# Hybrid conv / RG-LRU block: two output tiles on half the tokens at the start, the recurrence's factors in a PSUM bank, one subtraction on VectorE

## The chip, the cores and the metric

One core of a Trainium2 chip runs the whole kernel. The time is device microseconds (us) of one execution on that core. Engines are named as in the profile: PE is TensorE (matmuls), PEld its weight load, DVE VectorE, ACT ScalarE, POOL GpSimd, SP SyncE, which here only issues DMAs (SPq in the rows).

## The reference

A decoder block on 512 tokens of width 1024, in float32. Cut to what matters for the beginning of the kernel:

```python
h = rmsnorm(x, norm1_g)                      # 512 x 1024
z = h @ w_in + b_in                          # 1024 x 6656
z_glu, z_rx, z_rg, z_ga, z_gb = split(z, (2048, 1280, 1280, 1024, 1024))
u = z_glu[:, :1024] * sigmoid(z_glu[:, 1024:])          # then a causal convolution over 31 tokens
xb = causal_conv4(z_rx) ; r, i = sigmoid(gates of xb)
a = exp(-8 * r * softplus(-lru_lambda))      # 1280 channels, one lambda each
h_t = a * h_(t-1) + sqrt(1 - a^2) * i * xb   # the recurrence
# ... two output matrices, sigmoid merge, w_mix_out, residual, rmsnorm, SwiGLU, residual, rmsnorm
```

## The kernel before

Activations lie transposed, channels on the 128 partitions and the 512 tokens along a tile of one PSUM bank. Every float32 matrix is split in a high and a low part (fp32r), and a product is three matmuls: high by high, high by low, low by high. An output tile of `w_in` (128 channels) is 8 slices of the contraction times 3, so 24 matmuls; `mm3` issues them, and with `lo_last=True` the eight with the weight's low part come after the sixteen with its high part.

A weight tile is a *chunk* of 128x1024 (512 KB). `emit_chunk` issues its load on SP into one of 4 buffers `raw`, casts it to the high part (`copy`, ACT unless VectorE is named), and subtracts for the low part (`lo`, POOL for the chunks of `w_in`), both in one of 5 buffers `hl`. `emit_to(n)` emits all chunks up to number n. The chunks come in the order in which PE wants them: 0 and 1 are the two halves of the first gated unit (GLU) tile, 2 and 3 those of the second, 4 and 5 the first tiles of the recurrent branch.

The beginning stands in one block `manual_schedule`, in which PE, ACT, DVE and SP keep the order of the code; behind it a scheduler arranges the instructions. The 512 tokens are four blocks of 128, `x[0]` to `x[3]`. `norm1_rows(t)` norms one block: ACT squares and sums both halves, DVE scales the first sum (the "stats" operation, L544), ACT takes the root, DVE the reciprocal (L551) and multiplies the two halves of x by it (L588). `turn_half(.., hf, ..)` then turns 256 tokens (two blocks) channel by channel: two transposes on PE into a bank (`tx`, L567), the high part `h1..h` by ACT (L575), the low part `h1..l` by DVE (L576), 8 times. `early_mm(i, hf)` multiplies early output tile i with half hf of the tokens; `EARLY = 2` means two GLU tiles, of two chunks each, so four output tiles on 256 tokens at a time. Later tiles are taken by `in_mm` on all 512 tokens, with the same 24 matmuls, each twice as wide.

The per-channel parameters (13 of them: gains, biases, taps, `lru_lambda`) come as short rows, are turned by PE and copied by DVE into the tile `par`: `rows_turned(c0, c1)`, whose bank is `par_ps`. `ROWS` gives their order. From `lru_lambda` some 25 tiny DVE operations (128x10) and one exponential make the factors `c4`, `c8` of the recurrence, and two make `bh`.

DMAs of SP go over eight semaphores in turn, so each waits, before it is issued, until the one eight places ahead has landed; what stands behind it on SP waits too.

Of the kernel before, what the change touches and what calls it, by code (L numbers as in the profile page):

```python
# [22 lines left out]
LRU_C = 8.0  # L23
# [4 lines left out]
NR = DR // P  # L28
# [23 lines left out]


ROWS = [
    ("norm1_g", 8), ("b_in", 52), ("conv_dw_b", 8), ("conv_ln_g", 8), ("conv_ln_b", 8),
    ("conv_b_out", 8), ("lru_conv_b", 10), ("lru_ba", 10), ("lru_bx", 10),
    ("lru_lambda", 10), ("norm2_g", 8), ("lru_conv_w", 40),
    ("conv_dw_w", 248),
]


def gate_pieces():
# [24 lines left out]
def tile_block(ctx, tc, a, out):  # L87
    nc = tc.nc
    pool = lambda name, bufs, **k: ctx.enter_context(tc.tile_pool(name=name, bufs=bufs, **k))
    consts = pool("consts", 1)  # L90
# [30 lines left out]
    def split_to(h, l, full, eng, copy=act.copy):  # L121

        copy(h, full)  # L123
# [18 lines left out]
    def wchunk(key, src, kt, cols, where="hl", lo=pool_e, after=None):  # L142
        chunks.append((key, src, kt, cols, where, lo, after))

    def emit_chunk(copy=act.copy):
        if emitted[0] == GATES_AT:
            load_gates()
        key, src, kt, cols, where, lo, after = chunks[emitted[0]]
        emitted[0] += 1
        n = kt * cols  # L150
        if where == "made":
            raw = src()
        else:
            raw = raws.tile([P, 1024], F32, tag="raw", name=f"raw_{key}")
        rv = raw[:, :n]
        if where == "made":
            pass
        elif callable(src):
            src(raw)
        else:  # L160
            newest["load"] = nc.sync.dma_start(rv.rearrange("p (k n) -> p k n", k=kt), src).ins
# [12 lines left out]
    def emit_to(n, copy=act.copy):  # L174
        while emitted[0] < min(len(chunks), n):
            emit_chunk(copy)

    def weights(key, ahead=AHEAD):
        i = next(i for i, c in enumerate(chunks) if c[0] == key)
# [300 lines left out]
    xt = [[longt(f"x{t}{h}") for h in range(2)] for t in range(NT)]  # L480
# [26 lines left out]
    def rows_turned(c0, c1):  # L507
        pt = bank2(f"par_ps{c0}")
        for c in range(c0, c1, P):
            m = min(P, c1 - c)  # L510
            pe.transpose(pt[:, c - c0 : c - c0 + m], rowt[row_at(c)[0]][:m, :P], ident[:m, :m])
        vec.tensor_copy(par[:, c0:c1], pt[:, : c1 - c0])

    def pc(name, i):
        return par[:, col[name] + i : col[name] + i + 1]
# [22 lines left out]
    def rstd_begin(half, junk):  # L538

        i = n_stats[0]  # L540
        n_stats[0] += 1
        ss, r = stats[:, i, :2], stats[:, i, 2:3]
        act.activation(junk, half, AF.Square, accum_out=ss[:, 0:1])
        vec.tensor_scalar(out=ss[:, 0:1], in0=ss[:, 0:1], scalar1=1.0 / D, scalar2=EPS, op0=ALU.mult, op1=ALU.add)  # L544
        return ss, r
# [35 lines left out]

    h1p = [pairt(f"h1{c}") for c in range(ND)]

    def norm1_rows(t):
        junk = [shortt(f"n1j{t}{h}") for h in range(2)]
        r = rstd_of(xt[t], junk)
        for h in range(2):
            vec.tensor_scalar(out=xt[t][h], in0=xt[t][h], scalar1=r, scalar2=None, op0=ALU.mult)  # L588

    HALVES = [slice(0, 256), slice(256, 512)]  # L590
    EARLY = 2
    EARLY_IN = [(GLU + j + 8 * o) for j in range(EARLY) for o in range(2)]
    early = []

    def early_mm(i, hf):
        m = EARLY_IN[i]
        if hf == 0:
            early.append((m, w_tiles(f"in{m}", ND, 0), bank(f"z{m}")))
        _, ws, ps = early[i]
        mm3(ps[:, HALVES[hf]], ws, parts_of(h1p, HALVES[hf]), lo_last=hf == 0)  # L600


    ET = mybir.EngineType
    with tc.manual_schedule(engines={ET.PE, ET.Activation, ET.DVE, ET.SP}):
        norm1_rows(0)
        norm1_rows(1)
        rows_turned(0, ROWS[0][1])
        emit_to(1, vec.tensor_copy)
        turn_half("tx", xt, "norm1_g", h1p, 0, [bank, bank, bank, bank2])
        emit_to(2, vec.tensor_copy)  # L610
        load_x(2)
        load_x(3)
        for i in first[1:]:
            load_rows(i)
        norm1_rows(2)
# [12 lines left out]
        for i in range(4):  # L628
            early_mm(i, 1)
    h1 = parts_of(h1p)  # L630

    lam = par[:, col["lru_lambda"] : col["lru_lambda"] + NR]
    sm = consts.tile([P, 6, NR], F32, name="sm")
    ab, e, s, s2, po, c4 = (sm[:, i, :] for i in range(6))
    vec.tensor_scalar(out=e, in0=lam, scalar1=-1.0, scalar2=None, op0=ALU.mult)
    vec.tensor_tensor(out=ab, in0=lam, in1=e, op=ALU.max)
    vec.tensor_scalar(out=c4, in0=e, scalar1=0.0, scalar2=None, op0=ALU.max)
    act.activation(e, ab, AF.Exp, scale=-1.0)  # L640
    vec.tensor_scalar(out=s, in0=e, scalar1=2.0, scalar2=None, op0=ALU.add)
    vec.reciprocal(s, s)
    vec.tensor_tensor(out=s, in0=s, in1=e, op=ALU.mult)
    vec.tensor_tensor(out=s2, in0=s, in1=s, op=ALU.mult)
    n_terms = 9
    vec.tensor_scalar(out=po, in0=s2, scalar1=1.0 / (2 * n_terms - 1), scalar2=1.0 / (2 * n_terms - 3), op0=ALU.mult, op1=ALU.add)
    for k in range(n_terms - 3, -1, -1):
        vec.tensor_tensor(out=po, in0=po, in1=s2, op=ALU.mult)
        vec.tensor_scalar(out=po, in0=po, scalar1=1.0 / (2 * k + 1), scalar2=None, op0=ALU.add)
    vec.tensor_tensor(out=po, in0=po, in1=s, op=ALU.mult)  # L650
    vec.scalar_tensor_tensor(out=c4, in0=po, scalar=2.0, in1=c4, op0=ALU.mult, op1=ALU.add)

    c8 = consts.tile([P, NR], F32, name="c8")
    vec.tensor_scalar(out=c8, in0=c4, scalar1=-LRU_C / 2, scalar2=None, op0=ALU.mult)
    vec.tensor_scalar(out=c4, in0=c4, scalar1=-LRU_C / 4, scalar2=None, op0=ALU.mult)

    bh = consts.tile([P, 2, NR], F32, name="bh")
    for g, name in enumerate(("lru_ba", "lru_bx")):
        vec.tensor_scalar(out=bh[:, g, :], in0=par[:, col[name] : col[name] + NR], scalar1=0.5, scalar2=None, op0=ALU.mult)

    def b_in(m):
        return pc("b_in", m)
# [354 lines left out]
    def mix_end(second, plus, r1, r2, r7, third):  # L1017
# [10 lines left out]

        with tc.manual_schedule(engines={ET.PE, ET.Activation, ET.DVE}):
            second()  # L1030
# [251 lines left out]
```

## Time and profile before

| | |
|---|---|
| time, median of 3 runs | 800.91 us (800.60 to 801.02) |
| profiled execution: its own time / its span | 800.75 us / 799.0 us |
| PE busy | 790.3 us (99%) |
| DVE, ACT, POOL busy | 676.4 us (85%), 469.8 us (59%), 232.1 us (29%) |
| granted TensorE clock | 0.999 |

PE is busy for nearly the whole span, so the time is PE's work plus the few microseconds in which it has none: at the very start, while the first norm runs, and after its last matmul. The other engines matter where PE waits for them. A matmul's busy time in the rows is longer than its spacing, since matmuls are pipelined: what one costs is read from the start of one to the start of the next, or from the chain of waits, where a run of n matmuls stands with its length.

### The profile page before, as it was taken

How to read it: one execution, taken by the hardware profiler on the slowest of the kernel's cores; microseconds unless marked ns; L12 is line 12 of the kernel's file. 1: busy time of each engine (PE TensorE's matmuls, PEld its weight loads, DVE VectorE, ACT ScalarE, POOL GpSimd, SP SyncE). 2: the span in 40 equal slices, each digit the busy share in tenths (PEclk: the TensorE clock that was granted, in tenths of full speed). 3: DMA queues.
4: the chain of work that ended last, by engine and by line, in shares of the span. 5: the costliest groups of instructions: out<-in, count | busy, mean ns of one | idle time of the engine just before them, and what ended most of it. 6: DMA issues, size and time to landing. Idle time of an engine off the chain costs nothing.

```text
span 799.0 us, 12275 instructions
## 1 busy us (share of the span) xinstructions
PE 790.3 (99%) x4417; PEld 692.8 (87%) x4417; DVE 676.4 (85%) x1027; ACT 469.8 (59%) x681; POOL 232.1 (29%) x182
## 2 busy tenths in 40 slices
PE   8999999999999999999999999999999999999997
PEld 8988888888888888888888898999999999887885
DVE  6699899999989988795897889877878887889757
ACT  6446595897668854562335575545455555577443
POOL 3565867687765856130000000000000000000000
PEclk9999999999999999999999999999999999999999
DMA  7945557377664764357947545567655543676652
GB/s 222 229 122 167 171 152 211 121 222 212 179 198 138 220 183 129 129 190 231 297 172 251 172 132 158 126 162 189 159 132 134 132 132 106 205 264 204 197 172 106
DMA packets 184625, 140.31 MB, mean 176 GB/s; under 512 B 14279, under 2 KB 162163, under 8 KB 184563
## 3 DMA queue, kind: packets, MB, share of 16 engines
q1 hardware_dynamic: 183123, 134.27, 55.5%
q0 software_dynamic: 1440, 5.24, 3.5%
q8 instruction: 35, 0.57, 0.3%
q14 instruction: 27, 0.22, 0.1%
HBM read 113.79 MB, written 18.64 MB: 166 GB/s over the span
## 4 chain that ended last, share of the span: by engine, by line
PE 85%; DVE 6%; DMA 6%; issue 1%; SPq 1%; ACT 1%; DVEq 0%; POOLq 0%; ACTq 0%
PE z L527 35%; PE or L944 7%; PE yb L527 7%; PE fa L1071 6%; PE ft L1071 6%; PE ya L527 5%; PE mxr L944 5%; PE g L818 3%; PE fr L1071 3%; PE fe L1071 3%; PE fb L1071 2%; DMA raw_fb<-in_ffn_w_dram 2%; DMA raw_fb<-raw_fb 2%; PE f L527 1%; DVE hl_ob L119 1%
## 5 line engine op out<-in xcount | busy, mean ns | idle before, releaser
L693 DVE SCALAR_TENSOR_TENSOR cv<-u,par,cv 128x511 f32<-128x511 f32 (+16 forms) x240 | 162.0, 728 | 2.3 <-ACT cv L690 2.2
L119 POOL TENSOR_TENSOR hl_in<-raw_in,hl_in 128x1024 fp32r<-128x1024 f32 x52 | 126.4, 2436 | 82.5 <-ACT hl_in L123 67.3
L349 POOL DMA_DIRECT2D raw_fb<-raw_fb x10 | 8.8, 877 | 298.9 <-DVE raw_fb L351 187.8
L119 POOL TENSOR_TENSOR ows<-ows 128x256 f32<-128x256 f32 x66 | 57.2, 869 | 37.7 <-DMA ows<-in_ffn_w_dram 34.7
L123 ACT CAST hl_ft<-raw_fb 128x1024 fp32r<-128x1024 f32 x40 | 41.9, 1049 | 35.5 <-DVE raw_fb L351 20.4
L123 ACT CAST hl_in<-raw_in 128x1024 fp32r<-128x1024 f32 x48 | 50.0, 1041 | 10.7 <-PE z L527 6.6
L119 DVE TENSOR_TENSOR hl_ft<-raw_fb,hl_ft 128x1024 fp32r<-128x1024 f32 x40 | 48.5, 1218 | 7.5 <-ACT hl_ft L123 7.4
L119 DVE TENSOR_TENSOR hl_fb<-raw_fb,hl_fb 128x1024 fp32r<-128x1024 f32 x30 | 36.6, 1221 | 9.2 <-ACT hl_fb L123 8.8
L351 DVE TENSOR_TENSOR raw_fb<-raw_fb,raw_fb 128x1024 f32<-128x1024 f32 x20 | 24.5, 1224 | 21.2 <-DMA raw_fb<-in_ffn_w_dram 21.0
L527 PE MATMUL z<-h10h,hl_in 128*128 128x512 f32 (+1 forms) x112 | 42.2, 378 | 0.0
L527 PE MATMUL z<-h11h,hl_in 128*128 128x512 f32 (+1 forms) x112 | 41.7, 374 | 0.0
L527 PE MATMUL z<-h13h,hl_in 128*128 128x512 f32 (+1 forms) x112 | 41.7, 374 | 0.0
L527 PE MATMUL z<-h16h,hl_in 128*128 128x512 f32 (+1 forms) x112 | 41.7, 374 | 0.0
L527 PE MATMUL z<-h15h,hl_in 128*128 128x512 f32 (+1 forms) x112 | 41.7, 374 | 0.0
L527 PE MATMUL z<-h14h,hl_in 128*128 128x512 f32 (+1 forms) x112 | 41.7, 374 | 0.0
L527 PE MATMUL z<-h12h,hl_in 128*128 128x512 f32 (+1 forms) x112 | 41.7, 374 | 0.0
L527 PE MATMUL z<-h17h,hl_in 128*128 128x512 f32 (+1 forms) x112 | 41.7, 374 | 0.0
L123 ACT CAST hl_fb<-raw_fb 128x1024 fp32r<-128x1024 f32 x30 | 31.4, 1048 | 8.4 <-PE mxr L944 3.7
L123 ACT CAST hl_ob<-raw_ob 128x1024 fp32r<-128x1024 f32 (+1 forms) x23 | 23.4, 1015 | 21.7 <-PE or L944 10.9
L119 DVE TENSOR_TENSOR hl_ob<-raw_ob,hl_ob 128x1024 fp32r<-128x1024 f32 (+1 forms) x23 | 27.0, 1174 | 10.5 <-ACT hl_ob L123 7.7
L1071 PE MATMUL fe<-hs_0h,hl_ft 128*128 128x256 f32 x160 | 30.8, 284 | 0.1
L1071 PE MATMUL ft<-hs_1h,hl_ft 128*128 128x256 f32 x160 | 30.4, 283 | 0.0
(1015 smaller groups left out, 2625.4 us busy)
## 6 DMA issues: line engine op xcount, KB each, us to landing
raw_in<-in_w_in_dram SPq DMA_DIRECT2D x52, 512.0 KB
raw_fb<-in_ffn_w_dram SPq DMA_DIRECT2D x96, 256.0 KB
ows<-in_ffn_w_dram SPq DMA_DIRECT2D x44, 256.0 KB
os<-ows SPq DMA_DIRECT2D x22, 512.0 KB
raw_ob<-in_ffn_w_dram SPq DMA_DIRECT2D x33, 256.0 KB
raw_ot<-os SPq DMA_DIRECT2D x33, 256.0 KB
raw_lo<-in_lru_w_out_dram SPq DMA_DIRECT2D x16, 320.0 KB
raw_fb<-raw_fb POOLq DMA_DIRECT2D x10, 512.0 KB, 4.5
```

Source lines behind the costliest of these rows:

```text
L119: return eng.tensor_tensor(out=o, in0=x, in1=y, op=ALU.subtract)
L123: copy(h, full)
L349: pool_e.dma_start(out=q, in_=y, accum_op=ALU.add)
L351: vec.tensor_tensor(out=q, in0=q, in1=y, op=ALU.add)
L527: pe.matmul(ps, l, r, start=i == 0, stop=i == n - 1)
L693: vec.scalar_tensor_tensor(out=acc[c][:, s:], in0=u[c][:, : T - s], scalar=dw(c, s), in1=acc[c][:, s:], op0=ALU.mult, op1=ALU.add)
L818: pe.matmul(ps, l, r, start=k == 0, stop=k == len(mms) - 1)
L944: pe.matmul(banks[i], l_[:, ts], r_, start=start and n == 0, stop=stop and n == 2, skip_group_check=again)
L1071: pe.matmul(ps[:, HALVES[i]], lw[:, 4 * i + c, :], rx_, start=not (again or i or c or m), stop=bool(i and c == 3 and m == 2), skip_group_c ...
```

## The change

Five edits, all in the first 40 us:

1. `EARLY` is 1: only the two tiles of the first GLU tile are taken on half the tokens. Tiles 2 and 3 are taken later by `in_mm`, on all 512 tokens.
2. Chunks 2 and 3 are emitted later: `emit_to(3)` behind the second `turn_half`, `emit_to(4)` behind the factors, so their loads stand on SP behind all row loads, and their casts are ACT's, not DVE's.
3. The low part of chunk 1 is subtracted by VectorE, in the middle of block 2's norm (`Later` keeps the operands until `between` is called), not by POOL.
4. `ROWS` has `lru_lambda`, `b_in`, `lru_ba`, `lru_bx` ahead, and the first turned bank (`n_first`) holds these.
5. `lru_factors` makes `c4`, `c8` and `bh` right behind that bank's copy, with scratch in the free columns of the same PSUM bank, and a polynomial of 7 combined steps in place of 7 times two operations.

```diff
 ROWS = [
-    ("norm1_g", 8), ("b_in", 52), ("conv_dw_b", 8), ...
+    ("norm1_g", 8), ("lru_lambda", 10), ("b_in", 52), ("lru_ba", 10), ("lru_bx", 10),
+    ("conv_dw_b", 8), ...
 ]
+N_FIRST = 5
...
+    class Later:
+        def tensor_tensor(self, **operands):
+            self.operands = operands
...
-    def emit_chunk(copy=act.copy):
+    def emit_chunk(copy=act.copy, lo_by=None):
...
+        lo = lo_by or lo
...
-    n_first = ROWS[0][1] + ROWS[1][1]
+    n_first = sum(n for _, n in ROWS[:N_FIRST])
...
-    def norm1_rows(t):
+    def norm1_rows(t, between=None):
...
-        r = rstd_of(xt[t], junk)
+        r = rstd_of(xt[t], junk, between)
...
-    EARLY = 2
+    EARLY = 1
...
+    def lru_factors(scratch):
+        lam = par[:, col["lru_lambda"] : col["lru_lambda"] + NR]
+        e, q, po, cc = (scratch[:, i * NR : (i + 1) * NR] for i in range(4))
+        ab, s, s2 = (lru_t[:, i, :] for i in range(3))
...
+        act.activation(ab, ab, AF.Exp, scale=-1.0)
...
+        for k in range(n_terms - 2, 0, -1):
+            vec.scalar_tensor_tensor(out=po, in0=po, scalar=1.0 / (2 * k + 1), in1=s2, op0=ALU.add, op1=ALU.mult)
...
         emit_to(1, vec.tensor_copy)
         turn_half("tx", xt, "norm1_g", h1p, 0, [bank, bank, bank, bank2])
-        emit_to(2, vec.tensor_copy)
+        later = Later()
+        emit_to(2, vec.tensor_copy, later)
         load_x(2)
         load_x(3)
         for i in first[1:]:
             load_rows(i)
-        norm1_rows(2)
+        norm1_rows(2, lambda: vec.tensor_tensor(**later.operands))
         norm1_rows(3)
-        emit_to(4, vec.tensor_copy)
         for i in range(len(parts)):
             if i not in first:
                 load_rows(i)
         early_mm(0, 0)
         early_mm(1, 0)
         turn_half("tx", xt, "norm1_g", h1p, 1, [bank2, bank, bank])
-        early_mm(2, 0)
-        early_mm(3, 0)
-        rows_turned(ROWS[0][1], n_first)
+        emit_to(3)
+        early_mm(0, 1)
+        lru_factors(rows_turned(ROWS[0][1], n_first)[:, 2 * P :])
+        emit_to(4)
+        early_mm(1, 1)
         rows_turned(n_first, n_rows)
-        for i in range(4):
-            early_mm(i, 1)
...
-    for k in range(n_terms - 3, -1, -1):
-        vec.tensor_tensor(out=po, in0=po, in1=s2, op=ALU.mult)
-        vec.tensor_scalar(out=po, in0=po, scalar1=1.0 / (2 * k + 1), scalar2=None, op0=ALU.add)
...
```

How the instructions move is seen at three places. The first is VectorE during the norm of blocks 2 and 3 (`x_118` to `x_121` are their halves); before, from the cast of chunk 1 (`raw_in_247`) to the first low part of the second 256 tokens:

```order
L123 CAST hl_in_249<-raw_in_247 128x1024
L544 TENSOR_SCALAR stats<-stats 128x1
L551 RECIPROCAL stats<-stats 128x1
L588 TENSOR_SCALAR x_118<-x_118,stats 128x512
L588 TENSOR_SCALAR x_119<-x_119,stats 128x512
L544 TENSOR_SCALAR stats<-stats 128x1
L551 RECIPROCAL stats<-stats 128x1
L588 TENSOR_SCALAR x_120<-x_120,stats 128x512
L588 TENSOR_SCALAR x_121<-x_121,stats 128x512
L123 CAST hl_in_277<-raw_in_275 128x1024
L123 CAST hl_in_282<-raw_in_280 128x1024
L576 SCALAR_TENSOR_TENSOR h10l<-tx_348,par,h10h 128x256
```

The same stretch of VectorE after the change:

```order
L123 CAST hl_in_253<-raw_in_251 128x1024
L551 TENSOR_SCALAR stats<-stats 128x1
L652 TENSOR_TENSOR hl_in_253<-raw_in_251,hl_in_253 128x1024
L558 RECIPROCAL stats<-stats 128x1
L595 TENSOR_SCALAR x_118<-x_118,stats 128x512
L595 TENSOR_SCALAR x_119<-x_119,stats 128x512
L551 TENSOR_SCALAR stats<-stats 128x1
L558 RECIPROCAL stats<-stats 128x1
L595 TENSOR_SCALAR x_120<-x_120,stats 128x512
L595 TENSOR_SCALAR x_121<-x_121,stats 128x512
L583 SCALAR_TENSOR_TENSOR h10l<-tx_342,par,h10h 128x256
```

One subtraction (L652, chunk 1's low part) has come in ahead of the first reciprocal, and two casts (chunks 2 and 3) have gone from ahead of `h10l`.

The second place is PE from the last transposes of the second 256 tokens on; before (`z_388` is output tile 2, which needs a new bank):

```order
L567 MATMUL tx_383<-ident,x_119 128x128
L567 MATMUL tx_383<-ident,x_121 128x128
L527 MATMUL z_388<-h10h,hl_in_277 128x256
L527 MATMUL z_388<-h10l,hl_in_277 128x256
L527 MATMUL z_388<-h11h,hl_in_277 128x256
```

And after (`z_292` is output tile 0, whose bank it has held since its first half):

```order
L574 MATMUL tx_377<-ident,x_119 128x128
L574 MATMUL tx_377<-ident,x_121 128x128
L534 MATMUL z_292<-h10h,hl_in_208 128x256
L534 MATMUL z_292<-h10l,hl_in_208 128x256
L534 MATMUL z_292<-h10h,hl_in_208 128x256
L534 MATMUL z_292<-h11h,hl_in_208 128x256
```

What follows the transposes is now the second half of an old tile, in the order high-high, high-low, low-high for each slice, not the first half of a new one.

The third place is SP, the queue of the loads, before, from the last load of x on (`raw_in_275` and `raw_in_280` are chunks 2 and 3):

```order
L484 DMA x_121<-in_x_dram 128x512
L477 DMA rows_110<-in_b_in_dram 52x128
L161 DMA raw_in_275<-in_w_in_dram 128x8x128
L161 DMA raw_in_280<-in_w_in_dram 128x8x128
L477 DMA rows_111<-in_conv_dw_b_dram 8x128
```

After, from the last row loads on (`raw_in_382` and `raw_in_437` are chunks 2 and 3, `raw_in_476` is chunk 4; ahead of these rows stand eleven more row loads, which come right behind `x_121`):

```order
L483 DMA rows_111<-in_conv_dw_w_dram 38x128
L483 DMA rows_112<-in_conv_dw_w_dram 128x128
L483 DMA rows_113<-in_conv_dw_w_dram 82x128
L167 DMA raw_in_382<-in_w_in_dram 128x8x128
L167 DMA raw_in_437<-in_w_in_dram 128x8x128
L167 DMA raw_in_476<-in_w_in_dram 128x8x128
```

The two chunk loads have been moved behind 13 row loads, so that chunks 2, 3 and 4 are loaded one behind the other.

Behind the beginning the order is the same on PE, POOL and SP, but for two neighbours that change places on SP.

More of the change, by code (lines that the diff above doesn't have):

```diff
@@ L54 @@
 ROWS = [
[L55 to L58, printed above, removed]
+    ("norm1_g", 8), ("lru_lambda", 10), ("b_in", 52), ("lru_ba", 10), ("lru_bx", 10),
+    ("conv_dw_b", 8), ("conv_ln_g", 8), ("conv_ln_b", 8), ("conv_b_out", 8), ("lru_conv_b", 10),
+    ("norm2_g", 8), ("lru_conv_w", 40), ("conv_dw_w", 248),
 ]
+N_FIRST = 5
 def gate_pieces():
@@ L172, in emit_chunk, with emit_to @@
             ]
-    def emit_to(n, copy=act.copy):
+    def emit_to(n, copy=act.copy, lo_by=None):
         while emitted[0] < min(len(chunks), n):
-            emit_chunk(copy)
+            emit_chunk(copy, lo_by)
     def weights(key, ahead=AHEAD):
@@ L512, in rows_turned @@
         vec.tensor_copy(par[:, c0:c1], pt[:, : c1 - c0])
+        return pt
     def pc(name, i):
@@ L600, in early_mm @@
         mm3(ps[:, HALVES[hf]], ws, parts_of(h1p, HALVES[hf]), lo_last=hf == 0)
+    c4, c8 = (consts.tile([P, NR], F32, name=n) for n in ("c4", "c8"))
+    bh = consts.tile([P, 2, NR], F32, name="bh")
+    lru_t = consts.tile([P, 3, NR], F32, name="lru_t")
+    def lru_factors(scratch):
+        lam = par[:, col["lru_lambda"] : col["lru_lambda"] + NR]
+        e, q, po, cc = (scratch[:, i * NR : (i + 1) * NR] for i in range(4))
+        ab, s, s2 = (lru_t[:, i, :] for i in range(3))
+        vec.tensor_scalar(out=e, in0=lam, scalar1=-1.0, scalar2=None, op0=ALU.mult)
+        vec.tensor_tensor(out=ab, in0=lam, in1=e, op=ALU.max)
+        act.activation(ab, ab, AF.Exp, scale=-1.0)
+        for g, name in enumerate(("lru_ba", "lru_bx")):
+            vec.tensor_scalar(out=bh[:, g, :], in0=par[:, col[name] : col[name] + NR], scalar1=0.5, scalar2=None, op0=ALU.mult)
+        vec.tensor_scalar(out=q, in0=ab, scalar1=2.0, scalar2=None, op0=ALU.add)
+        vec.reciprocal(q, q)
+        vec.tensor_tensor(out=s, in0=q, in1=ab, op=ALU.mult)
+        vec.tensor_tensor(out=q, in0=q, in1=s, op=ALU.mult)
+        vec.tensor_tensor(out=s2, in0=q, in1=ab, op=ALU.mult)
+        n_terms = 9
+        vec.tensor_scalar(out=po, in0=s2, scalar1=1.0 / (2 * n_terms - 1), scalar2=None, op0=ALU.mult)
+        for k in range(n_terms - 2, 0, -1):
+            vec.scalar_tensor_tensor(out=po, in0=po, scalar=1.0 / (2 * k + 1), in1=s2, op0=ALU.add, op1=ALU.mult)
+        vec.scalar_tensor_tensor(out=s, in0=po, scalar=1.0, in1=s, op0=ALU.add, op1=ALU.mult)
+        vec.tensor_scalar(out=e, in0=e, scalar1=0.0, scalar2=0.5, op0=ALU.max, op1=ALU.mult)
+        vec.tensor_tensor(out=cc, in0=e, in1=s, op=ALU.add)
+        vec.tensor_scalar(out=c8, in0=cc, scalar1=-LRU_C, scalar2=None, op0=ALU.mult)
+        vec.tensor_scalar(out=c4, in0=cc, scalar1=-LRU_C / 2, scalar2=None, op0=ALU.mult)
     ET = mybir.EngineType
@@ L623, in tile_block @@
         turn_half("tx", xt, "norm1_g", h1p, 1, [bank2, bank, bank])
-        early_mm(2, 0)
-        early_mm(3, 0)
-        rows_turned(ROWS[0][1], n_first)
+        emit_to(3)
[3 more added lines that the diff above has]
+        early_mm(1, 1)
         rows_turned(n_first, n_rows)
-        for i in range(4):
-            early_mm(i, 1)
     h1 = parts_of(h1p)
[L634 to L646, printed above, removed]
-    for k in range(n_terms - 3, -1, -1):
-        vec.tensor_tensor(out=po, in0=po, in1=s2, op=ALU.mult)
[L649 to L659, printed above, removed]
     def b_in(m):
```

## The prediction

> **What bounds the kernel now.** I read the chain of work that ended last first. In order of time it stands, for the first 130 us, as start, length and what:
>
> ```profile
> 14.09 2.48 DVE x L588 x2
> ...
> 18.13 1.20 DVE hl_in L123 x2
> 19.34 0.41 DVE h10l L576
> ...
> 19.79 0.83 PE tx L567 x4
> 20.61 5.97 PE z L527 x48
> 26.59 0.66 PE par_ps L511 x4
> 27.24 44.19 PE z L527 x240
> ```
>
> Up to 19.7 us the chain runs through the norm on VectorE; from 20.6 us on it is PE and nothing else. The same chain later, where PE's rate in full tiles is seen:
>
> ```profile
> 245.97 65.30 PE z L527 x288
> ...
> 456.39 0.87 PE th L567 x8
> ...
> 480.79 10.24 PE f L527 x45
> 491.05 1.06 ACT hl_fb L123
> ...
> 543.43 3.13 PE fr L1071 x24
> ```
>
> The third view is that of the waits, for PE over the whole span (total, times, longest):
>
> ```profile
> PE fr L1071 <- ACT ft L1171: 0.6, 1, 0.6
> PE tx L567 <- DVE h10l L576: 0.6, 1, 0.6
> PE tx L567 <- DVE x L588: 0.5, 1, 0.5
> ```
>
> The first is at 543 us; the other two are those before the chain becomes PE's. After 20.6 us PE waits no longer than that 0.6 us for anyone until its last matmul. So whatever brings PE's continuous work forward by d brings the end forward by d, unless some wait opens later. The change lies in the stretch of the other two, 1.1 us together. The question is when PE begins output tile 4, the first tile that both kernels treat alike. Before, its first matmul is the first of 512 columns, in the timeline:
>
> ```profile
> 38.60 0.40 PE L527 MATMUL z<-h10h,hl_in 128*128 128x512 f32 x1
> ```
>
> So the sum is 38.60 us less the start of tile 4 after the change.
>
> **Part A: the second half's start.** The timeline of the norm of blocks 2 and 3 (start, busy):
>
> ```profile
> 9.66 2.39 POOL L119 TENSOR_TENSOR hl_in<-raw_in,hl_in 128x1024 fp32r<-128x1024 f32 x1 [8.35 <-DVE hl_in L123]
> ...
> 13.32 0.15 DVE L544 TENSOR_SCALAR stats<-stats 128x1 f32<-128x1 f32 x1
> ...
> 13.49 2.40 POOL L119 TENSOR_TENSOR hl_in<-raw_in,hl_in 128x1024 fp32r<-128x1024 f32 x1 [1.44 <-DVE stats L544]
> ...
> 13.89 0.16 DVE L551 RECIPROCAL stats<-stats 128x1 f32<-128x1 f32 x1 [0.42 <-ACT stats L550]
> ...
> 14.09 2.08 DVE L588 TENSOR_SCALAR x<-x,stats 128x512 f32<-128x512 f32 x1
> ...
> 15.96 0.36 PE L527 MATMUL z<-h10h,hl_in 128*128 128x256 f32 x1
> ...
> 16.49 0.14 DVE L544 TENSOR_SCALAR stats<-stats 128x1 f32<-128x1 f32 x1
> ...
> 17.00 0.27 PE L567 MATMUL tx<-ident,x 128*128 128x128 f32 x1
> ...
> 17.25 0.88 DVE L588 TENSOR_SCALAR x<-x,stats 128x512 f32<-128x512 f32 x2
> ...
> 17.79 1.42 PE L567 MATMUL tx<-ident,x 128*128 128x128 f32 x11 [0.52 <-DVE x L588]
> ...
> 18.16 0.48 ACT L575 ACTIVATE h10h<-tx,par 128x256 fp32r<-128x256 f32 x1 [1.14 <-PE tx L567]
> ...
> 19.25 0.48 DVE L576 SCALAR_TENSOR_TENSOR h10l<-tx,par,h10h 128x256 fp32r<-128x256 f32 x1
> ...
> 19.65 0.47 DVE L576 SCALAR_TENSOR_TENSOR h11l<-tx,par,h11h 128x256 fp32r<-128x256 f32 x1
> ...
> 20.17 0.20 PEld L567 LDWEIGHTS tx<-ident,x 128*128 128x128 f32 x2 [0.19 <-DVE h11l L576]
> ...
> 20.57 0.19 PEld L527 LDWEIGHTS z<-h10h,hl_in 128*128 128x128 f32 x1 [0.19 <-DVE h12l L576]
> ```
>
> The scaling at 14.09 takes 2.08 us where its like take half of 0.88: it ends 0.3 us after POOL's subtraction of chunk 1 (13.49 + 2.40 = 15.89). With that subtraction taken off POOL, the stall of 1.6 us goes. In its place DVE does the subtraction itself. Its price is that of the same form elsewhere:
>
> ```profile
> L119 DVE TENSOR_TENSOR hl_ft<-raw_fb,hl_ft 128x1024 fp32r<-128x1024 f32 x40 | 48.5, 1218 | 7.5 <-ACT hl_ft L123 7.4
> ```
>
> The Trainium skill ("SBUF — State Buffer", section "Who interferes with whom") says that VectorE and GpSimd share one pair of ports as an exclusive lock, and that a VectorE instruction with two SBUF inputs contends with a GpSimd one that reads SBUF; the 2.08 us agree with a lock, and by this rule the new subtraction could itself be locked out if POOL were busy.
>
> Step by step: the statistics operation stands at 13.32 as before, and its successor starts at 13.48. The subtraction ends about 14.7 (13.48 + 1.22). Root and reciprocal have been waiting; x is scaled from 14.9 (0.20 behind the reciprocal's start, as 13.89 to 14.09) to 15.7. The next statistics follow, and 0.76 us later (16.49 to 17.25) block 3 is scaled, from 16.42. PE ends the first half of tile 1 at 17.00, as before; its 0.5 us wait for x is gone. The first pair of transposes is done 0.7 us earlier, so ACT starts `h10h` at 17.48 (0.37 behind the transpose, as 17.79 to 18.16) and DVE `h10l` at 18.0. Before it stood at 19.25, for the two casts of chunks 2 and 3 (1.20 us in the chain) came first; they are gone to ACT.
>
> From there as before: the last transposes wait for `h11l`, which is 0.40 behind `h10l` and lasts 0.47; they begin at 18.9 (before 20.17, which is 0.92 behind `h10l`). The first matmul before also waited for `h12l`, whose bank the new tile took. Tile 0 has its bank already, so it follows the four-transpose rate at once: two transposes of 0.12 give 19.15. **A = 20.57 - 19.15 = 1.4 us.** A lower bound: were the subtraction as slow as POOL's 2.40, A would lose 1.2 and be 0.2. An upper bound is PE itself: 16 transposes from 17.00 at the `th` rate of 0.109 (0.87 over 8) end at 18.75, so 1.8. I take 1.4, which is made of rows of the same operations. DVE's low parts then come 0.39 us apart and PE wants one each 0.36 us but starts 1.2 us after the first; it never catches up within 8 (0.03 x 8 = 0.24).
>
> **Part B: two tiles whole.** Before, 4 tiles x 2 halves x 24 matmuls have 256 columns. Of the chain's 240 matmuls in 44.19 us, 144 are of 512 columns at 65.30 / 288 = 0.2267, so 32.65; the other 96 take 11.54, 0.1203 each. A pair of halves costs 0.2405 and a whole one 0.2267, so 0.0138 us are saved for each of the 48 matmuls of tiles 2 and 3: **B = 0.66 us.**
>
> The Trainium skill ("TensorE: Matmul & The Clock Gate", section "Back-to-back issue gap") gives a warm gap of N / 2.4 + 2.5 ns, 109.2 ns for 256 columns and 215.8 for 512, hence 2.5 ns a pair and 0.12 us in all. The trace's 120.3 and 226.7 do not agree with either figure.
>
> **Part C: the parameters' transposes are in two places.** Four of them cost 0.66 us in one place, against 0.44 at the `th` rate, so entering and leaving costs about 0.2 us. A second place costs between 0 (the `th` transposes stand between matmuls without any extra) and 0.22; I take **C = -0.15 us.**
>
> **What must stay hidden.** The factors are tiny operations on DVE. Before, they held DVE until the first GLU result at 37.9:
>
> ```profile
> 31.53 2.26 DVE L649 TENSOR_SCALAR sm<-sm 128x10 f32<-128x10 f32 x1
> ...
> 37.87 0.74 DVE L757 SCALAR_TENSOR_TENSOR u<-z,par,sg 128x512 f32<-128x512 f32 x1
> ```
>
> That cost PE nothing, and now they start at about 22 us, so DVE is only earlier, some 10 us. Queued behind them on DVE is the copy of the other parameters, wanted by ACT and DVE alone. Cost zero; with that cover gone, PE's seventh tile would wait for the bank that `u` frees, not before 47.6 us (36.7 and two tiles of 5.44). Chunk 1's low part is ready at 14.7, and PE wants it at 15.96 (the first matmul with a low part of tile 1), as before.
>
> Chunk 2 is the one with a due time. Its subtraction is still POOL's (2.40), behind a cast on ACT (1.05). On SP:
>
> ```profile
> 10.36 2.73 SPq L477 DMA_DIRECT2D rows<-in_conv_dw_b_dram  x1
> 13.13 0.30 SPq L477 DMA_DIRECT2D rows<-in_conv_ln_g_dram  x1
> 13.47 0.30 SPq L477 DMA_DIRECT2D rows<-in_conv_ln_b_dram  x1
> ...
> 17.76 1.17 SPq L477 DMA_DIRECT2D rows<-in_conv_dw_w_dram  x3
> 19.05 1.01 SPq L161 DMA_DIRECT2D raw_in<-in_w_in_dram  x2
> ...
> 22.89 1.05 ACT L123 CAST hl_in<-raw_in 128x1024 fp32r<-128x1024 f32 x1 [1.70 <-DMA raw_in<-in_w_in_dram]
> ```
>
> SP's wait until 13.1 is for chunk 1's landing, eight places ahead. After the change that wait stands before `lru_bx`; behind it come 8 row loads at 0.34 (13.13 to 13.47) and the three of the taps (1.2), so chunk 2 is issued at 13.1 + 2.7 + 1.2 = 17.0 at the latest. Chunk 4 before needed 3.84 us from issue to use (19.05 to 22.89), so chunk 2 lands by 20.9, is cast by 22.0 and subtracted by 24.4. PE comes to it at 19.15 + 5.8 (two half tiles) + 0.8 (parameters) = 25.7 and wants the low part at the third matmul, 26.2. There are 1.8 us in hand. Chunk 3 has 5.4 us more, for a cast and a subtraction behind the exponential.
>
> **The sum.** 1.4 + 0.66 - 0.15 = 1.9 us. Tile 4 starts at 36.7 instead of 38.60. The profiled execution goes from 800.75 (span 799.0) to 798.85; the median of the runs is 0.16 above it, so 800.91 - 1.9 = **799.0 us**. About 0.2% (1.6 us) is what a measurement of this kernel can tell from no change; the forecast is a little over it.
>
> **The rivals.**
>
> *Chunk 2 late (slower).* PE stands still at the first GLU tile's successor until the low part comes. If chunk 2 lands at L, the part is ready at L + 3.5; PE loses L + 3.5 - 26.2. That begins at L = 22.7, eats the gain at 24.6 and makes the kernel slower by over 0.2% from 26.2. For it: row loads wait in turn for loads eight places ahead, and one such wait lasted 2.7 us before. A second and a third of that size give L = 26.4, a loss of 3.7 and 802.7 us. Against it: every load before a wait is short, and no chunk is among them now. Chance 0.07.
>
> *The stall only changes its owner.* DVE's subtraction takes 2.4 us, by a lock or otherwise, and block 3 is scaled no earlier: A falls to 0.2, the sum to 0.7, the time to 800.2. Against it: POOL's first subtraction ends at 12.05 (9.66 + 2.39) and it has no other until chunk 2. Chance 0.09.
>
> *The gain is lost in the middle.* From 491 to 543 us the chain leaves PE and runs through DVE and DMAs, with PE only 0.6 us behind. If that stretch were paced by the DMAs alone, PE would wait there for what it gained: 800.9. Against it: the stretch begins with ACT's cast right at the end of PE's matmuls at 491.05, so it moves along. Chance 0.11.
>
> *Halves cost no more than wholes,* by the gap formula cited: worked with 2.5 ns a pair, B is 0.12, the sum 1.4, the time 799.5. The rows speak against it. Chance 0.03.
>
> **How the numbers follow.** The forecast has 0.70. Within it A, B and C can come out 0.4 lower or higher; I put 0.62 of it beyond 0.2% and 0.08 within. Same: 0.08 + 0.09 + 0.10 + 0.03 = 0.30. Slower: 0.07 + 0.01 (the middle lost with interest) = 0.08. The range goes from 798.3 (A at its bound of 1.8 and C at 0 give 2.5) to 800.3 (the stall kept gives 800.2); it leaves out the late chunk and the middle.
>
> **What would show it.** Right: the subtraction on DVE at 13.5 for 1.2; the scaling of x at 14.9 in 0.9; `h10l` at 18.0; the first matmul of the second half at 19.15; the third tile without a wait; the first matmul of tile 4 at 36.7. Wrong: a wait of PE for POOL's or ACT's `hl_in` near 26 us, a chain that leaves PE between 20 and 490 us, or a longer wait than 0.6 at 543.

## The result, and the profile after

The changed kernel takes 798.06 us (median of 9 runs, 797.33 to 798.77), the kernel before 800.60 in the same series (9 runs). The ratio is 0.9968, with a 95% interval of 0.9958 to 0.9978, which is a gain of 1.8 to 3.4 us. The median's gain is 2.54 us where 1.9 was forecast, and the time lies 0.24 us under the lower end of the range. The profiled execution's own time is 797.70 us.

The head of the page after:

```profile
span 795.9 us, 12177 instructions
PE 789.2 (99%) x4369; PEld 690.5 (87%) x4369; DVE 673.2 (85%) x1020; ACT 471.7 (59%) x683; POOL 228.8 (29%) x181
```

The span is 3.1 us shorter, PE's busy time only 1.1 us (790.3 before): two thirds of the gain is time in which PE stood still. The waits of PE after (total, times, longest) are this one line:

```profile
PE warm L506 <- DVE ones L499: 1.1, 1, 1.1
```

The two waits ahead of the second half's transposes (0.6 and 0.5 us) are gone, as forecast, and so are two late ones (0.6 at 543 us and 0.2), whose going the forecast did not count on. The chain of waits after, from the warm-up to tile 4 and beyond:

```profile
1.09 7.80 PE warm L506 x42
8.89 0.15 PE par_ps L517
9.04 1.90 PE tx L574 x16
10.94 6.51 PE z L534 x48
17.45 2.13 PE tx L574 x16
19.58 2.87 PE z L534 x24
22.44 0.07 PE par_ps L517
22.52 2.92 PE z L534 x24
25.43 0.29 PE par_ps L517 x3
```

It is PE's from the warm-up on; VectorE has no place in it any more between 8.9 and 25.7 us. VectorE's timeline in the norm of blocks 2 and 3 (start, busy):

```profile
13.82 1.23 DVE L652 TENSOR_TENSOR hl_in<-raw_in,hl_in 128x1024 fp32r<-128x1024 f32 x1
...
15.15 0.88 DVE L595 TENSOR_SCALAR x<-x,stats 128x512 f32<-128x512 f32 x2
...
16.72 0.88 DVE L595 TENSOR_SCALAR x<-x,stats 128x512 f32<-128x512 f32 x2
18.21 0.48 DVE L583 SCALAR_TENSOR_TENSOR h10l<-tx,par,h10h 128x256 fp32r<-128x256 f32 x1 [0.61 <-ACT h10h L582]
```

The subtraction costs 1.23, both scalings 0.88, and nothing stands ahead of `h10l` but ACT's high part. Chunk 2's way through SP, ACT and POOL:

```profile
15.55 4.79 SPq L167 DMA_DIRECT2D raw_in<-in_w_in_dram  x4
20.57 1.10 ACT L123 CAST hl_in<-raw_in 128x1024 fp32r<-128x1024 f32 x1
21.74 2.39 POOL L119 TENSOR_TENSOR hl_in<-raw_in,hl_in 128x1024 fp32r<-128x1024 f32 x1 [9.41 <-ACT hl_in L123]
```

It is issued at 15.55 (bound: 17.0), ACT takes it at 20.57 with no idle time ahead (the casts of `h1` were what it had to do first), and its low part is ready at 24.13. PE's timeline from the second half on:

```profile
17.28 2.30 PE L574 MATMUL tx<-ident,x 128*128 128x128 f32 x16
19.33 0.36 PE L534 MATMUL z<-h10h,hl_in 128*128 128x256 f32 x1
...
22.16 0.28 PE L534 MATMUL z<-h17h,hl_in 128*128 128x256 f32 x1
...
22.51 0.28 PE L534 MATMUL z<-h10l,hl_in 128*128 128x256 f32 x1
...
25.15 0.28 PE L534 MATMUL z<-h17h,hl_in 128*128 128x256 f32 x1
25.27 0.46 PE L517 MATMUL par_ps<-ident,rows 128*128 128x128 f32 x3
25.52 0.47 PE L534 MATMUL z<-h10h,hl_in 128*128 128x512 f32 x1
25.83 0.39 PE L534 MATMUL z<-h10l,hl_in 128*128 128x512 f32 x1
26.06 0.40 PE L534 MATMUL z<-h10h,hl_in 128*128 128x512 f32 x1
...
36.51 0.39 PE L534 MATMUL z<-h10h,hl_in 128*128 128x512 f32 x1
```

Third tile at 25.52 without a wait; its low part is wanted at 26.06, 1.9 us after it was ready; tile 4 at 36.51 (forecast 36.7).

**An anchor.** Single starts mislead, though, since PE's first output matmul, F, moves from execution to execution: before at 10.18 and after at 10.70 in the two profiles above. With six more profiles there are four of each kernel; their means are these. F2 is the first matmul of the second half, T4 that of tile 4.

| | F | F to F2 | F2 to T4 | T4 to the span's end | span |
|---|---|---|---|---|---|
| before, 4 profiles | 10.20 | 10.32 | 18.03 | 760.23 | 798.78 |
| after, 4 profiles | 10.22 | 8.76 | 17.18 | 759.45 | 795.60 |
| difference | 0.02 | -1.56 | -0.85 | -0.78 | -3.18 |

F2 to T4 repeats to 0.02 us, F to F2 to 0.2. So the start gave 2.4 us, and 0.78 more came behind tile 4. The spans differ by 3.2 where the medians of the runs differ by 2.5 in the first series and by 2.8 and 3.1 in two later ones (below); the first series' interval holds all of these.

### The profile page after: what moved, and what is told of

Same layout as the page of the kernel before. It is cut to its first block, busy times and chain, and to the rows that moved or that the text cites. A ratio compares the mean times of both kernels' runs of the same rounds, so it can differ in the third digit from the quotient of the medians.

```text
span 795.9 us, 12177 instructions
## 1 busy us (share of the span) xinstructions
PE 789.2 (99%) x4369; PEld 690.5 (87%) x4369; DVE 673.2 (85%) x1020; ACT 471.7 (59%) x683; POOL 228.8 (29%) x181
## 4 chain that ended last, share of the span: by engine, by line
PE 99%; DVE 0%; issue 0%; ACT 0%
PE z L534 36%; PE or L953 13%; PE ft L1080 7%; PE yb L534 7%; PE fa L1080 7%; PE fr L1080 6%; PE ya L534 5%; PE mxr L953 5%; PE fe L1080 4%; PE g L827 3%; PE fb L1080 2%; PE f L534 2%; PE warm L506 1%; PE f L1106 1%; PE tx L574 1%; PE th L574 0%
## 5 line engine op out<-in xcount | busy, mean ns | idle before, releaser
L702 DVE SCALAR_TENSOR_TENSOR cv<-u,par,cv 128x511 f32<-128x511 f32 (+19 forms) x240 | 162.4, 730 | 5.0 <-ACT cv L699 4.7
L119 POOL TENSOR_TENSOR hl_in<-raw_in,hl_in 128x1024 fp32r<-128x1024 f32 x51 | 123.5, 2426 | 83.1 <-ACT hl_in L123 69.6
L123 ACT CAST hl_in<-raw_in 128x1024 fp32r<-128x1024 f32 x50 | 52.1, 1043 | 10.4 <-PE z L534 6.6
```

The lines of the kernel that those rows point to most:

```text
L119: return eng.tensor_tensor(out=o, in0=x, in1=y, op=ALU.subtract)
L702: vec.scalar_tensor_tensor(out=acc[c][:, s:], in0=u[c][:, : T - s], scalar=dw(c, s), in1=acc[c][:, s:], op0=ALU.mult, op1=ALU.add)
```

## The experiments

**The same two kernels again.** Run and profiled again, they give the table above and its spread. In one series the changed kernel took 797.61 against 800.45 (ratio 0.9962, interval 0.9950 to 0.9974), in another 797.53 against 800.59 (0.9958, 0.9945 to 0.9971).

> The changed kernel once more, for a second profile beside the three that follow. Theory 1: the whole gain is made before output tile 4, whose first matmul stood at 36.51 us after the change against 38.60 before; PE's warm-up happened to last until 8.89 us in that profile against 8.28, so with an equal warm-up the gain there is 2.1 + 0.4 = 2.5 us, and the two late waits of PE in the profile of before (0.6 us at 543, 0.2 at 736) are chance. Then the start of tile 4 here lies between 36.0 and 36.6 in step with the warm-up's end, the ratio to before is again near 0.9968, and a late wait of PE may show. Theory 2: about 0.9 us of the gain is made late, because DVE is ahead and those waits are gone for good: none here either, and the part from tile 4 to PE's last matmul is 0.9 us shorter than before's in every profile.

> The changed kernel again, on the same chip as the two with more work on VectorE, for their comparison and as a fourth profile: tile 4 25.8 to 26.0 us behind the first output matmul, the low part of xb7 134.7 behind tile 4, no wait for ext6h; the ratio to before between 0.9962 and 0.9968.

Four more profiled executions, three of the kernel before and one of the changed kernel:

> The kernel before once more, for a second profile. Counted from PE's first matmul of an output tile (10.18 us in the first profile), tile 4 must start 28.4 us later again. Theory 1 (late waits are chance): PE's wait of 0.6 us at 543 us for ACT's copy may be absent or of another size. Theory 2 (the change takes it away): the wait is there again with 0.4 to 0.8 us, and the stretch from the first fr to the first fb matmul, 108.7 us in the first profile against 107.8 in four profiles of changed kernels, is again above 108.3.

> The kernel before, a third profile: two things stay open, whether PE's late waits (0.8 and 0.5 us in two profiles) are its own or chance, and whether its first output matmul at 10.15 us is earlier than the changed kernel's 10.4 to 10.7 for a reason. If both are chance, a late wait anywhere from 0 to 1.1 us and a first matmul anywhere from 10.1 to 11.1; tile 4 is 28.4 us behind it in any case.

> The changed kernel, a third profile, for the same two questions: tile 4 is 25.8 to 26.0 us behind the first output matmul in any case; if the late waits are chance, one of up to 1 us may show, as the run with fewer warm-up matmuls had one of 1.1 us; if the change takes them away, none.

> The kernel before, a fourth profile, for the same two questions and with the same expectation.

They took 800.41, 800.45, 797.03 and 800.55 us. In these three profiles of before, the late wait stood at another place than at 543 us. The shortest and the longest of them, from two views of the waits (0.6 in the third):

```profile
PE g L818 <- DMA ext6h<-xb7h: 0.5, 1, 0.5
```

```profile
PE g L818 <- DMA ext6h<-xb7h: 0.7, 1, 0.7
```

PE waits there, at some 183 us, for the DMA that rearranges the last slice of the recurrent branch (`xb7`) for the gates' matmuls. Every profile of before has one late wait of 0.5 to 0.7, here or at 543; none of the four after has any. That is most of the 0.78. The two places are not alike: the one at 543 shows in one of the four profiles of before, and it shows again in variants of the changed kernel (0.3 to 1.1 us, below), so the change has not closed it for good.

**Edit 3 undone: chunk 1's low part by POOL again.**

```diff
-        later = Later()
-        emit_to(2, vec.tensor_copy, later)
+        emit_to(2, vec.tensor_copy)
...
-        norm1_rows(2, lambda: vec.tensor_tensor(**later.operands))
+        norm1_rows(2)
```

> The changed kernel with the low part of chunk 1 on POOL again (edit 3 undone). Theory 1: the stall of DVE's scaling is back (2.08 us in place of 0.44), block 3 is scaled some 0.5 us later, the second half starts at about 19.9 with a warm-up as in the first profile after (19.33 there), and the time is 0.5 to 0.6 us above the changed kernel's, 0.9975 of before. Rival: PE is the bound of the second half's start, so the stall is hidden and nothing changes (0.9968).

798.75 us (8 runs; ratio 0.9976, 0.9966 to 0.9986). POOL's timeline, and below it VectorE's:

```profile
14.42 2.40 POOL L119 TENSOR_TENSOR hl_in<-raw_in,hl_in 128x1024 fp32r<-128x1024 f32 x1 [1.44 <-DVE stats L551]
```

```profile
15.02 2.48 DVE L595 TENSOR_SCALAR x<-x,stats 128x512 f32<-128x512 f32 x2
```

The two scalings take 2.48 instead of 0.88, and the pair's end is 0.7 behind POOL's, as before. F to F2 is 9.62, 0.86 more than after. So edit 3 is worth 0.86 us there (0.5 to 0.6 was expected), and what the rows show of it is the stall. The Trainium skill ("SBUF — State Buffer", "Who interferes with whom") has VectorE in a two-port mode and GpSimd exclude each other, and whoever issues first hold the shared ports for its whole instruction. The trace agrees with the order, POOL having started 0.6 us before the scaling; the mode of the scaling stands in no row.

**Edit 3 alone,** put into the kernel before:

```diff
-        emit_to(2, vec.tensor_copy)
+        later = Later()
+        emit_to(2, vec.tensor_copy, later)
...
-        norm1_rows(2)
+        norm1_rows(2, lambda: vec.tensor_tensor(**later.operands))
```

> The kernel before with edit 3 alone: the low part of chunk 1 by VectorE in block 2's norm. In the changed kernel, undoing this edit cost 0.92 us up to tile 4. Theory 1: the scaling is no longer stalled, block 3 is scaled 0.7 to 0.8 us earlier, the two casts that stay on VectorE follow at once, and tile 4 starts 27.6 to 27.7 us behind the first output matmul instead of 28.4; the time is 0.8 us below before's (0.9990). Rival: the casts of chunks 2 and 3 now meet POOL's subtraction or the later order moves, and nothing is left of it (1.0000).

799.07 us (11 runs) against 800.16; 0.9986 (0.9977 to 0.9995). VectorE again:

```profile
13.29 1.22 DVE L621 TENSOR_TENSOR hl_in<-raw_in,hl_in 128x1024 fp32r<-128x1024 f32 x1
...
14.62 0.88 DVE L593 TENSOR_SCALAR x<-x,stats 128x512 f32<-128x512 f32 x2
```

F to F2 falls from 10.32 to 9.54, and F2 to T4 stays at 18.02. The edit brings 0.78 when done alone and 0.86 when undone alone. PE's wait for `ext6h` is 0.2 us here.

**Edit 2 undone: chunks 2 and 3 early, cast by VectorE.**

```diff
         norm1_rows(3)
+        emit_to(4, vec.tensor_copy)
...
-        emit_to(3)
...
-        emit_to(4)
```

> The changed kernel with the loads of chunks 2 and 3 back at their old place on SP and their casts on DVE ahead of the second low parts (edit 2 undone). Theory 1: the two casts (1.20 us) stand ahead of h10l again, which had waited 0.61 us for ACT, so it starts 0.6 us later and so does the second half; the time is 0.6 us above the changed kernel's, 0.9975 of before. Rival: the early loads and casts are worth having, since chunk 2 stands ready: no loss, 0.9968 or below.

805.36 us (5 runs): 1.0058 (1.0046 to 1.0070), slower than the kernel before. PE's timeline and, below it, its longest wait:

```profile
19.01 0.83 PE L574 MATMUL tx<-ident,x 128*128 128x128 f32 x4 [0.48 <-DVE h10l L583]
19.60 0.36 PE L534 MATMUL z<-h10h,hl_in 128*128 128x256 f32 x1
```

```profile
PE g L826 <- DMA ext6h<-xb7h: 3.3, 1, 3.3
```

At the start it costs about what was expected (0.6): F to F2 is 9.29, 0.53 more. The last four transposes take 0.59 to the first matmul, against 0.78 before (19.79 to 20.57), for tile 0 has its bank: 0.19 for that. So 0.86 + 0.53 + 0.19 = 1.58 accounts for all of the 1.56 from F to F2. Most of the loss is elsewhere: 3.3 us of waiting at 184 us, for the DMA of `xb7h`, and what that wait does to PE's clock (last section).

**Edit 1's core undone: tiles 2 and 3 in halves again.**

```diff
-    EARLY = 1
+    EARLY = 2
...
         rows_turned(n_first, n_rows)
+        for hf in range(2):
+            early_mm(2, hf)
+            early_mm(3, hf)
```

> The changed kernel with output tiles 2 and 3 taken on two halves of the tokens as before, but at their new place behind all else (the core of edit 1 undone: 96 matmuls of 256 columns for 48 of 512). By the prediction's rows (0.1203 and 0.2267 us) tile 4 starts 0.66 us later than in the changed kernel, and the time is 0.66 us longer, 0.9976 of before. By the cited gap formula 0.12 us, 0.9969. If halves cost nothing at all: no difference.

798.40 us (12 runs); 0.9977 (0.9968 to 0.9985). F to F2 is 8.79, as after (8.76); F2 to T4 is 17.78, so the halves cost 0.60. The forecast took 0.66 from the chain's rows; the 0.12 by the gap formula is not what these matmuls show. The Trainium skill ("TensorE: Matmul & The Clock Gate", "Back-to-back issue gap") gives that formula for an isolated matmul, and says that in a stream of matmuls with weight loads both set the spacing, which the prediction left out. PE waits again for `ext6h`, 0.4 us.

**One place for all transposes of parameters.**

```diff
-        lru_factors(rows_turned(ROWS[0][1], n_first)[:, 2 * P :])
         emit_to(4)
         early_mm(1, 1)
+        first_bank = rows_turned(ROWS[0][1], n_first)
         rows_turned(n_first, n_rows)
+        lru_factors(first_bank[:, 2 * P :])
```

> The changed kernel with all four transposes of the parameters in one place again, behind the second tile's second half, and the factors behind them. In the changed kernel the two places cost 0.11 and 0.33 us, in the kernel before the one place cost 0.66. Theory 1: four transposes in one place cost 0.4 to 0.5 wherever they stand, and the 0.66 of before is due to its place behind the eight low-part matmuls: no difference in time (0.1 at most). Rival: one place costs 0.66 here too, because the bank or the rows are waited for, so tile 4 starts 0.2 us later. The prediction's own sum would have it 0.15 earlier.

798.90 us (10 runs); 0.9978 (0.9969 to 0.9987). F2 to T4 is 17.14 against 17.18: a second place costs 0.04 us. The time it lost lies late:

```profile
PE g L828 <- ACT ext L803: 1.1, 1, 1.1
```

**The factors late,** behind the block, as before the change, with all else kept:

```diff
-        lru_factors(rows_turned(ROWS[0][1], n_first)[:, 2 * P :])
+        first_bank = rows_turned(ROWS[0][1], n_first)
...
+    lru_factors(first_bank[:, 2 * P :])
```

> The changed kernel with the factors made behind the whole beginning, as before, still in the bank (half of edit 5 undone; the order of the parameters stays). Theory 1: they were never waited for, so tile 4 starts at the same time, 25.9 us behind PE's first output matmul, and if the scheduler's later order holds, the time is that of the changed kernel. Rival: the factors' place sets the order that the scheduler makes of VectorE's side work, as in the run in which 294 rows of VectorE moved, and then PE waits between 70 and 250 us and the time is up to 6 us longer.

805.31 us (5 runs); 1.0065 (1.0051 to 1.0079). ACT's timeline, and the two long waits of PE behind the warm-up:

```profile
20.37 1.28 ACT L621 ACT_TABLE_LOAD   x1
22.88 0.21 ACT L621 ACTIVATE lru_t<-lru_t 128x10 f32<-128x10 f32 x1 [1.23 <-DVE lru_t L620]
23.00 1.03 ACT L123 CAST hl_in<-raw_in 128x1024 fp32r<-128x1024 f32 x1
```

```profile
PE g L828 <- DMA ext8l<-xb7l: 4.7, 1, 4.7
...
PE z L534 <- POOL hl_in L119: 0.7, 1, 0.7
```

Outside the block the scheduler put the exponential ahead of chunk 2's cast on ACT; the cast starts at 23.00, not 20.57, and PE waits 0.7 for POOL's low part: F2 to T4 is 18.15, and the expectation that tile 4 would start at the same time was wrong. This is the forecast's late chunk, by another road: not the load but ACT's queue. The rest is the late wait again.

**Why these two lost so much.** In the order of VectorE's instructions, 122 convolution steps (`cv`) stand ahead of the subtraction that makes `xb7`'s low part: in before, in after and in seven of the experiments. In the two that lost, 133 do. From the groups of the page after:

```profile
L702 DVE SCALAR_TENSOR_TENSOR cv<-u,par,cv 128x511 f32<-128x511 f32 (+19 forms) x240 | 162.4, 730 | 5.0 <-ACT cv L699 4.7
```

Eleven steps at 162.4 / 240 = 0.68 are 7.4 us of VectorE. From F, `xb7`'s low part comes 7.5 us later than after with the late factors and 5.7 later with the casts on VectorE. The scheduler took the convolution first; by which of its rules, no run shows. Since before has 122 too, without either edit, this is no gain of the change: it is what half the change would have cost.

**A shorter warm-up,** tried for more: `WARM = 17` in place of 21 (the rows count two matmuls for each).

> The changed kernel with 17 warm-up matmuls in place of 21. In two of four profiles of changed kernels PE's warm-up lasted until 8.9 us, and x had been ready by 8.3 to 8.8; in the others it ended at 7.9 and PE waited for x. Theory 1: with 17 PE always waits for x, the first output matmul starts at 10.2 to 10.4 us, and the time is 0.1 to 0.2 us below the changed kernel's on the mean, with less spread. Rival: the clock is not yet granted in full after 17, the first transposes run slower, and the time is 0.3 us or more above it.

798.54 us (7 runs); 0.9971 (0.9959 to 0.9982). Nothing came of it. At the start PE only waits for x (the second row). The first row is the wait at the place of before's 0.6 (here at 542 us), in a kernel that differs from the changed one in nothing but four warm-up matmuls:

```profile
PE fr L1080 <- ACT ft L1180: 1.1, 1, 1.1
...
PE tx L574 <- DVE x L595: 1.0, 1, 1.0
```

**VectorE held back behind tile 4,** to test whether its being earlier is what took the late waits away. Two or three operations whose result nobody uses:

```diff
+        if j == 2:
+            dummy = shortt("dummy")
+            for _ in range(2):          # 3 in the second kernel
+                vec.scalar_tensor_tensor(out=dummy, in0=uj, scalar=1.0, in1=uj, op0=ALU.mult, op1=ALU.add)
```

> The changed kernel with two more operations on VectorE in the third GLU tile (128x512, two inputs in SBUF, result unused), some 1.4 us of VectorE's time at about 70 us; the number of convolution steps ahead of the low part of xb7 stays 122. In ten profiles that low part stood 136.1 us behind the start of tile 4 where PE waited for the load of ext6h at 182 us (before, tiles in halves), and 134.7 where it did not (the changed kernel). Theory 1: VectorE's lead of 1.4 us is what takes the late wait away, so here it stands at 136.1 again and PE waits 0.4 to 0.7 us for ext6h; the time is 0.5 to 0.8 us above the changed kernel's of this call. Rival: the wait comes from SP's queue or the DMAs, not from VectorE, and the time does not change.

> The same with three such operations, 2.1 us. Theory 1: the low part of xb7 at 136.8 behind tile 4, PE waits 1.1 to 1.4 us for ext6h, the time is 1.2 to 1.6 us above the changed kernel's. Rival: no change.

797.49 us (6 runs; 0.9961, 0.9946 to 0.9975) and 797.75 (5 runs; 0.9962, 0.9949 to 0.9975), against 0.9958 for the changed kernel in the same series. `xb7`'s low part moved from 134.7 us behind T4 to 136.0 and 136.2, which is where before has it (136.1 to 136.2), and no wait for `ext6h` came back. So an earlier low part is not the cause, as the rival had it. (With three operations PE waits 0.3 us at the other late place, `fr`.) What stands closer to it: SP issues the load `ext6h` 138.2 us behind T4 in the changed kernel and 138.3 and 138.4 in these two, 138.8 to 139.0 in before, in the first profile as

```profile
177.51 0.54 SPq L798 DMA_DIRECT2D ext6h<-xb7h  x1
```

Its source is the high part, which ACT makes, and it stands in SP's queue behind other loads. ACT and SP with two operations:

```profile
171.48 0.62 ACT L123 CAST xb7h<-xb 128x512 fp32r<-128x512 f32 x1 [1.27 <-DVE xb L784]
...
173.98 0.59 SPq L444 DMA_DIRECT2D os<-ows  x1
174.99 0.54 SPq L811 DMA_DIRECT2D ext6h<-xb7h  x1
```

The high part starts 134.8 behind T4 here, against 133.5 after and 134.9 to 135.0 before, and the load is issued early all the same, so it is not the source that holds it. It is the queue: ahead of `ext6h` stands the store `os<-ows`, which SP issues as soon as POOL's last subtraction for `ows` ends. SP issues it 137.2 behind T4 in all four profiles after and 137.8 to 138.0 in the four before, and `ext6h` follows 1.0 later in all eight. Ahead of these subtractions POOL stands idle for 0.4 to 0.6 us in the four profiles of before, until a cast of ACT is done, and not at all in those after. Why that cast comes later in before is left open.

## Why the prediction was right, and where it was not

*Direction and the mechanism up to tile 4: right.* PE's time after 20 us was the bound, the 1.1 us of waits went, and the chain is PE's. The interval's upper end of 0.9978 lies beyond 0.2%.

*Part A: right in its steps, 0.16 short.* Forecast 1.4, measured 1.56 from F. The subtraction cost 1.23 (forecast 1.22), the scaling 0.88. Edit 3 carries 0.86, edit 2 0.53, the held bank 0.19. Of the shortfall 0.1 is the transposes: 16 took 2.05 to the first matmul (17.28 to 19.33) where 2.15 was worked out (17.00 to 19.15).

*Part B: right.* 0.66 forecast, 0.60 measured; 0.12, the rival by the gap formula, is out.

*Part C: wrong sign.* F2 to T4 gained 0.85, of which B is 0.60, so C is +0.25, not -0.15. The rows before show what the step took for its price:

```profile
26.31 0.28 PE L527 MATMUL z<-h17h,hl_in 128*128 128x256 f32 x1
26.52 0.73 PE L511 MATMUL par_ps<-ident,rows 52*128 52x52 f32 x4
...
27.21 0.28 PE L527 MATMUL z<-h10l,hl_in 128*128 128x256 f32 x1
```

From the last `z` ahead to the second behind it is 0.90, less two spacings of 0.12: 0.66. After, the two places cost 0.35 - 0.24 = 0.11 and 0.68 - 0.12 - 0.23 = 0.33, together 0.44, by the same reading; with one place for all (above) 0.41. So the price lay not in the number of places but in something of that one place before, which no run isolates. The step divided one price into work and entering, and charged the entering twice.

*What must stay hidden: chunk 2 right, "cost zero" wrong.* Chunk 2 had 1.9 us in hand (forecast 1.8); PE waited neither for SP's eight places nor for the lock. But the factors and the casts were valued only up to tile 4. Their place also sets the order behind it: moved back, each costs about 8 us (ratios of 1.0058 and 1.0065 against 0.9962), most of it at 184 us. That the order of the changed kernel was the good one is luck: no step of the forecast bears on it.

*The step that failed: nothing behind tile 4.* "Whatever brings PE's work forward by d brings the end forward by d, unless some wait opens later" left out that a late wait can close. The 0.6 at 543 us was seen, and used only as something that might grow. So the sum had no term for what comes behind T4, and the range no bound for it; 0.78 was measured there, most of it PE's late wait, and the traces lead that wait at 183 us back to SP's queue and POOL. The second step is the sign of C, -0.15 for +0.25. Together they are why 798.3 was too high an end: 1.9 + 0.16 - 0.06 + 0.40 = 2.4 up to T4, and 0.78 behind it.

*How far outside is partly chance.* The forecast counts down from 800.91, the median of three runs; in the series of the result the kernel before took 800.60. Counted from there the range would end at 798.0, and 798.06 would lie inside it. The end itself was set a little wide: A at 1.8, B at 0.66 and C at 0 make 2.5, which is 798.4.

*The rivals.* The late chunk, the stall that changes its owner, and the gain lost in the middle: the trace after shows none of the three. The middle did cost PE 1.1 us in the kernel with the shorter warm-up.

## What to carry to other kernels

Measure a change at the start from an anchor that it leaves alone (here the first output matmul), and split what comes behind it from what the change itself does: here 2.4 us and 0.8. Where a wait late in the trace is short but there, give it a bound downward too, since an earlier or differently ordered side stream can take it away as well as make it grow. Where a scheduler arranges what comes behind a hand-written block, look at the order of the side engines ahead of the next narrow place: eleven steps on VectorE were worth more than the whole edit.

## What the runs showed of the hardware

A wait of PE of 3.3 us cost more than its length. In the kernel with the casts back on VectorE, three windows show PE's wait for `ext6h` and what follows (window, length, busy time of PE, PEld, DVE, ACT and POOL with instructions, granted clock, DMA share, GB/s):

```profile
181.00:184.40 3.40, 0.16 (x1) 0.00 (x0) 3.40 (x7) 3.29 (x5) 1.69 (x1) 1.00 1.03 282
184.40:185.40 1.00, 0.92 (x3) 0.62 (x4) 1.00 (x2) 0.01 (x1) 1.00 (x2) 1.00 1.12 197
185.40:188.90 3.50, 3.50 (x11) 2.68 (x10) 3.33 (x6) 3.15 (x4) 3.26 (x5) 0.51 1.00 253
```

After 3.3 us without work PE goes on at full clock for 1 us, and then has a granted clock of 0.51 for 3.5 us. Matmuls of 512 columns come 0.43 apart there, not 0.23:

```profile
186.76 0.63 PE L826 MATMUL g<-ext6h,hl_gate 112*128 112x512 f32 x1
187.19 0.63 PE L826 MATMUL g<-ext6l,hl_gate 112*128 112x512 f32 x1
```

Eight of them cost 8 x 0.20 = 1.6 us more, half of the wait again. With 0.53 at the start, 3.3 and two more waits of 0.3 this makes 6.0 of the 6.8 us by which this span (802.4) is over the 795.6 of after. The Trainium skill ("TensorE: Matmul & The Clock Gate", "Part 1: The HAM clock gate (the "warmup" mystery)") has the clock halved after an idle window of about 3.4 us. Here a wait of 3.3 us was enough, while behind the waits of 0.5 to 0.7 in before the granted clock stays at 1.00. The two kernels with a wait over 1.1 us (3.3 and 4.7) are also the only ones with a mean granted clock of 0.996; all others have 0.998 to 1.000.

PE's first 42 matmuls, on constant data, took from 6.57 to 7.80 us in profiles of one and the same kernel, and F moved from 9.69 to 10.70: with them in three of the four profiles, while in the fourth PE waited 0.4 us for x behind 6.88 us of warm-up. The row of the chain of another profile of the changed kernel, beside the 7.80 above:

```profile
1.09 6.57 PE warm L506 x42
```

Of the five operations that held VectorE back (128x512, two inputs in SBUF) three took 0.67 us, and one in each kernel 2.62: it started 0.3 us into a subtraction of POOL of 2.40 and ended 0.5 us behind it. That is the size of stall that edit 3 takes away, here at a place where nobody waited for it.
